# Attention of a two-layer decoder trunk: the join of two head groups in two later parts, weight casts tied behind attention casts, long scans placed behind a turn

## The chip, the cores and the metric

The kernel runs on one core of one Trainium2 chip. The metric is the device time of one execution in microseconds; the number for the kernel before is the median of three runs.

## What is computed

Two layers; each adds to the residual stream x (1024 tokens, 1024 features) first a mixer and then a gated feed-forward part, and a final normalisation follows. All arithmetic is float32.

```python
h = rmsnorm(x, norm1[l]); proj = h @ w_in[l]
qa, ka, va, qb, kb, vb, gate_pre = jnp.split(proj, splits, axis=-1)
o_a = dilated_mixture(...)            # 3 groups of 4 heads of 64: windows 128, 512, 2048, dilations 1, 4, 16
o_b = stick_breaking_attention(...)   # 4 heads of 64
gates = jax.nn.sigmoid(gate_pre + b_gate[l])
merged = g_a * (o_a @ w_br[l, :OUT_A]) + g_b * (o_b @ w_br[l, OUT_A:])
x = x + merged @ w_o[l]
h2 = rmsnorm(x, norm2[l]); up = h2 @ w_up[l]; a, v = up[..., :D_FF], up[..., D_FF:]
x = x + (gelu(causal_depthwise_conv(a)) * v) @ w_down[l]
```

Per head slot the three groups of the first mixer are combined with weights proportional to their softmax denominators. The stick-breaking attention weighs key s for query t with sigmoid(z_ts) times the product of (1 - sigmoid(z_tj)) over all j between s and t; a query block of 128 rows needs a scan along its keys.

## The kernel before

**Products.** A float32 operand is split into a high part (a cast on ACT, line 130) and a low part (source less high part, on DVE, line 135); `split` does both. A product takes three matmuls: high by high, high by low, low by high. The larger projections (`pair`, `up`, `down`) use seven block products instead of eight; their weight sums are made on POOL and DVE and split by `piece`. In `pair` the sums are called w1 to w7, and one step of the generator (a "share") is six matmuls, half of one block product.

**Orders.** PE executes in the order of the program text. For ACT, DVE, POOL and the DMA queue of SP a planner chooses the order when the program is built: it takes what it thinks ready, by priority, which falls in program order; `tc.high_priority(offset=AHEAD)` moves instructions 200 places ahead, and a dependency NO_SYNC fixes the order of two instructions of one engine. Then each engine executes its list strictly in order. `split(..., "is")` remembers the cast just made in `LAST["act"]`, and `split(..., "waits")` puts a cast behind the one remembered. Attention casts are "is" (through `parts`); the casts of the block sums of h are "waits".

**Attention among dense products.** `Dense` holds the dense products of the mixer; `attend` goes through 36 attention items and after each of their steps lets `dense.advance(rate)` issue a number of shares. `dense.at(n, f)` calls f after n more shares. An item has scores, and then pairs of a turn (PE transposes attention weights into a bank of the tag "t", `parts` casts them) and an apply (PE multiplies them with the values into a bank of "o"); `fold` adds the two halves of an o bank into SBUF. The scores of the next item are placed among the turns and applies of the current one, every `gap` places. Every tag of PSUM banks (ps, s, t, o) has two banks.

- B items (`stick_item`), 16 per layer, named by pair and index: two score blocks of up to 128x1024, a scan (line 639) and a product (line 640) for each, before the first turn.
- N items (`near_item`), 4 per layer: group of dilation 1.
- T items (`far_item`), 16 per layer: the two dilated groups, fused; `score` does a bias-and-minimum on DVE (line 807) and an Exp on ACT (line 808).

**Join.** When the last T item of a pair of heads is applied, `join(pr)` runs at once: 16 transposes spread the factors `fx` over four banks (two of "t", then two of "o"), and DVE does six 128x512 operations (lines 882 to 884) to combine the near and the far outputs in `on`. After the second join the remaining dense shares run (`dense.finish`), then the branch products (`br_ps`) with their gates (`gin`, line 1275); the output weights, then the branch weights, go through the two buffers of the tag "wr".

Of the kernel before, what the change touches and what calls it, by code (L numbers as in the profile page):

```python
# [15 lines left out]
P = 128  # L16
# [29 lines left out]
AHEAD_B = 3  # L46
X_AT = (3, 5, 7, 9)
AHEAD = 200


def f32(ap):
# [4 lines left out]
def trunk_kernel(ctx, tc, x, norm1, w_in, b_gate, w_br, w_o, norm2, w_up, conv_w, conv_b, w_down, norm_f, out, depth=None, probe=None):  # L56
# [70 lines left out]
    def split(hi, lo, src, turn=None):  # L127


        one = act.copy(hi, src)  # L130
# [4 lines left out]
        dve.tensor_tensor(lo, src, f32(hi), ALU.subtract)  # L135


    def weights(src, cols, place=None):
# [177 lines left out]
    def attend(dense, items):  # L316

        late = None  # L320
        for i, (name, first, rest, rate, make) in enumerate(items):
            if i == 0:
                dense.until(first)
                dense.step()
                dense.step()
                sc, micro = make()
                for f in sc:
                    f()
                    dense.advance(rate)
                dense.done.add(name + "s")  # L330
            dense.until(rest)
            seq = []
            for m, (t, p) in enumerate(micro):
                seq.append(t)
                if m == 0 and late:
                    seq.append(late)
                if m >= 1:
                    seq.append(micro[m - 1][1])

            def late(f=micro[-1][1], name=name):  # L340
                f()
# [12 lines left out]
            if pending or i + 1 == len(items):  # L354
                seq.append(late)
                late = None
            gap = max(1.0, len(seq) * 0.7 / max(1, len(nxt)))
            at = 0.0
            for j, f in enumerate(seq):
                if nxt and j >= at:  # L360
                    nxt.pop(0)()
                    at += gap
                    if not nxt:
                        dense.done.add(items[i + 1][0] + "s")
                    dense.advance(rate)
# [12 lines left out]
            micro = nmicro  # L378
# [233 lines left out]
            dve.tensor_tensor(dst, o[0:64, :], tmp[0:64, :n], ALU.add)  # L612


    def stick_item(pr, s, qp):
        if "ob" not in R:
            R["ob"] = big("ob")
        q, k, vt, ob = R["qb", pr], R["kb", pr], R["vb"], R["ob"]
        hd = 2 * pr + s
        rows, st, shared = {}, {}, {}  # L620

        def score(a):
            i = 2 * qp + a
            L = P * (i + 1)
            bt = rows[a] = sb.tile([P, T], F32, tag="p4", bufs=4, name="beta")
            if a == 0:
                st[0] = big("stay")
            sv = st[0][:, a, :]
            for c0 in range(0, L, 512):
                w = min(512, L - c0)  # L630
                z = bank("s", "z")
                scores(z[:, :w], *(t[:, s, i * P : i * P + P] for t in q), k[:, s, c0 : c0 + w])
                with tc.high_priority(offset=AHEAD):
                    if c0 + w == L:
                        dve.tensor_tensor(z[:, w - P : w], z[:, w - P : w], mask_b, ALU.add)
                    act.activation(bt[:, c0 : c0 + w], z[:, :w], AF.Sigmoid)
                    act.activation(sv[:, c0 : c0 + w], z[:, :w], AF.Sigmoid, scale=-1.0)  # L637
            rev = sv[:, 0:L][:, ::-1]
            dve.tensor_tensor_scan(rev, rev, zero[:, 0:1].to_broadcast([P, L]), 1.0, ALU.mult, ALU.add)  # L639
            dve.tensor_tensor(bt[:, 0 : L - 1], bt[:, 0 : L - 1], sv[:, 1:L], ALU.mult)  # L640

        def blocks(kb):

            return [(j, a) for j in range(2) for a in range(2) if kb + j <= 2 * qp + a]

        def turn(kb):
            tp = bank("t", "sb_t")
            todo = blocks(kb)
            for c, (j, a) in enumerate(todo):
                pe.transpose(tp[:, c * P : c * P + P], rows[a][:, (kb + j) * P : (kb + j + 1) * P], ident)  # L650
            shared[kb] = parts(tp, len(todo) * P, "sb")

        def apply(kb):
            last = kb == 2 * qp
            if kb == 0:
                shared["o"] = bank("o", "sb_o")[:, :256]
            o = shared["o"]
            for j in range(2):
                c = P if last and j else 0
                for p in (0, 1):  # L660
                    pe.matmul(
                        o[:, c:256],
                        vt[(kb + j) // 4][:, (kb + j) % 4, hd, :],
                        shared[kb][p][:, 256 * j : 256 * j + 256 - c],
                        start=(kb == 0 and j == 0 and p == 0),
                        stop=(last and j == 1 and p == 1),
                        skip_group_check=True,
                    )
# [106 lines left out]
    def far_item(dense, pr, s, r, share):  # L775
# [8 lines left out]
        def score():  # L784
# [15 lines left out]
            for n in range(2):  # L800
                flat = pt[:, 256:768] if n else pt[:, 0:256]
                if n:
                    zz, pp, bb = z1, flat, bias.rearrange("p g c -> p (g c)")
                else:
                    zz, pp, bb = z0[:, 0:256].rearrange("p (g c) -> p g c", g=2), flat.rearrange("p (g c) -> p g c", g=2), bias[:, :, P:256]
                nm = st[:, 0, s, n, r : r + 1]
                dve.tensor_tensor_reduce(pp, zz, bb, 1.0, 3e38, ALU.add, ALU.min, nm)
                act.activation(flat, flat, AF.Exp, bias=nm, scale=-1.0, accum_out=st[:, 1, s, n, r : r + 1])
            if (s, r) == (1, 3):
                factors(pr)  # L810

# [8 lines left out]
        def apply(g):  # L820
# [9 lines left out]
            if r % 2 == 1 and g == 1:  # L830
# [1 line left out]
                    R["ot", pr] = sb.tile([P, T], F32, tag="ot", name="ot")  # L832
                fold(R["ot", pr][64 * s : 64 * s + 64, 512 * (r // 2) : 512 * (r // 2) + 512], o)
                if s == 1 and r == 3:
                    join(pr)

        return [score], [(lambda g=g: turn(g), lambda g=g: apply(g)) for g in range(2)]

# [26 lines left out]
                pool.tensor_copy(fx[:, :, :, s, :], f[:, a, s, :, :].unsqueeze(3).to_broadcast([P, 2, 4, 64]))  # L865
            R["fx", pr].append(fx.rearrange("p n r s c -> p n r (s c)"))

    def join(pr):

        fx, on, ot = R["fx", pr], R["on"], R["ot", pr]  # L870
        spread = []
        for n in range(2):
            for a in range(2):
                o = bank("to"[n], "j_ps")
                for r in range(4):
                    pe.transpose(o[:, r * P : (r + 1) * P], fx[a][:, n, r, :], ident)
                spread.append(o.rearrange("p (r j) -> p r j", r=4))
        mine = on[:, pr, :].rearrange("p (n j r) -> p n r j", n=2, r=4)
        other = ot.rearrange("p (r n j) -> p n r j", r=4, n=2)
        for n in range(2):  # L880
            t = small("jn").rearrange("p (r j) -> p r j", r=4)
            dve.tensor_tensor(t, other[:, n], spread[2 * n + 1], ALU.mult)
            dve.tensor_tensor(mine[:, n], mine[:, n], spread[2 * n], ALU.mult)
            dve.tensor_tensor(mine[:, n], mine[:, n], t, ALU.add)


    def half(n, k):
        return [(H[n][0][:, 4 * k + i, :], H[n][1][:, 4 * k + i, :]) for i in range(4)]

    def piece(src):  # L890
        hi = sb.tile([P, 512], F32R, tag="wh", bufs=4, name="w_hi")
        lo = sb.tile([P, 512], F32R, tag="wl", bufs=4, name="w_lo")
        split(hi, lo, src)
        return hi, lo

    def seven(o, w, b, first, last):
# [65 lines left out]
    def pair(dense, l, offs, tiled, put):  # L962
# [23 lines left out]
        w1 = piece(a11)  # L986
        yield
        dve.tensor_tensor(a11, a21, a11, ALU.subtract)
        w5 = piece(a21)
        yield  # L990
        w6 = piece(a11)
        yield
        pool.tensor_tensor(a11, a12, a11, ALU.subtract)
# [932 lines left out]
```

## Time and profile before

| | |
|---|---|
| median of three runs | 2705.64 us (2704.53 to 2706.54) |
| the profiled execution | 2705.66 us, its span 2703.6 us |
| PE busy | 2663.9 us, 99% |
| PEld, DVE, ACT, POOL busy | 83%, 74%, 50%, 25% |
| mean granted clock of PE | 0.996 |

The page groups instructions by line, engine and tiles ("out<-in"); "idle before, releaser" tells how long the engine sat idle before them and whose end released it. PEld is PE's load of the stationary operand. An L number is a line of the kernel. In the waits, a row is: who waited <- for whom: us in total, times, longest. In a timeline, a row is: start, duration, engine, line, operation, tiles, shapes, count, and in brackets the idle time before it. The two layers run the same program, the second some 1340 us after the first, so most rows of the attention come twice.

### The profile page before, as it was taken

The numbers are of one execution on the slowest core, as the hardware profiler recorded it, in microseconds if no ns is written. First come the engines' busy times: TensorE is split into PE (matmuls) and PEld (weight loads), VectorE is DVE, ScalarE is ACT, GpSimd is POOL, SyncE is SP. The second block draws the span as 40 slices with busy tenths as digits, with TensorE's granted clock in tenths as the row PEclk, the third lists the DMA queues.
The fourth block names the chain that finished last, engine by engine and source line by source line (L and its number), as shares of the span: only waits on it lengthen the run. The fifth ranks groups of instructions, "written<-read, shape, count | busy, mean of one in ns | idle before, by whom it ended". The sixth has DMA issues, their size and how long they took to land.

```text
span 2703.6 us, 36629 instructions
## 1 busy us (share of the span) xinstructions
PE 2663.9 (99%) x13104; PEld 2236.2 (83%) x13104; DVE 2012.4 (74%) x2974; ACT 1351.8 (50%) x2494; POOL 673.2 (25%) x487
## 2 busy tenths in 40 slices
PE   9999999999999999999999999999999999999999
PEld 8988888888888888888888888888788888888888
DVE  5776855675789988897657767466848888988865
ACT  5655645464555555532335556455635555454225
POOL 1003221122233434321120042211311433343210
PEclk9999999999999999999999999999999999999999
DMA  5112178563235444688411122784722443446863
GB/s 161 32 52 94 45 192 244 190 234 110 86 117 171 141 156 142 221 324 315 167 36 40 48 90 75 206 250 162 251 86 78 151 160 136 169 145 252 335 244 122
DMA packets 358690, 421.05 MB, mean 156 GB/s; under 512 B 20732, under 2 KB 287340, under 8 KB 356972
## 3 DMA queue, kind: packets, MB, share of 16 engines
q1 hardware_dynamic: 358508, 418.70, 46.7%
q8 instruction: 104, 1.70, 0.3%
q14 instruction: 78, 0.64, 0.1%
HBM read 278.59 MB, written 140.05 MB: 155 GB/s over the span
## 4 chain that ended last, share of the span: by engine, by line
PE 82%; DVE 10%; issue 2%; ACT 2%; DMA 1%; POOL 1%; SPq 0%; DVEq 0%; POOLq 0%; ACTq 0%
PE u_a L899 5%; PE u_a L901 5%; PE u_a L900 5%; PE d_ps L1622 4%; PE d_ps L1624 4%; PE d_ps L1623 4%; PE u_c L901 3%; PE u_c L899 3%; PE u_c L900 3%; PE o_ps L160 2%; PE o_ps L162 2%; PE o_ps L161 2%; PE i_a L899 2%; PE i_a L900 2%; PE i_a L901 2%
## 5 line engine op out<-in xcount | busy, mean ns | idle before, releaser
L135 DVE TENSOR_TENSOR w_lo<-up_a,w_hi 128x512 fp32r<-128x512 f32 x240 | 237.6, 997 | 21.3 <-ACT w_hi L130 21.3
L130 ACT CAST w_hi<-up_a 128x512 fp32r<-128x512 f32 x240 | 149.4, 622 | 185.2 <-PE u_a L900 45.3
L1630 DVE TENSOR_TENSOR x<-x,d_ps 128x512 f32<-128x512 f32 (+1 forms) x228 | 152.0, 672 | 77.7 <-PE d_ps L1624 76.4
L1361 POOL TENSOR_TENSOR cv<-cv 128x512 f32<-128x512 f32 x88 | 132.3, 1515 | 249.4 <-DVE cv L1356 139.6
L135 DVE TENSOR_TENSOR g<-cv,g 128x512 fp32r<-128x512 f32 x154 | 152.6, 992 | 5.3 <-ACT g L130 2.7
L135 DVE TENSOR_TENSOR w_lo<-w_raw,w_hi 128x512 fp32r<-128x512 f32 x148 | 112.2, 761 | 58.0 <-ACT w_hi L130 57.4
L130 ACT CAST w_hi<-w_raw 128x512 fp32r<-128x512 f32 x148 | 91.9, 621 | 121.7 <-PE o_ps L161 69.7
L135 DVE TENSOR_TENSOR w_lo<-in_a,w_hi 128x512 fp32r<-128x512 f32 x120 | 86.1, 718 | 70.5 <-ACT w_hi L130 70.1
L130 ACT CAST w_hi<-in_a 128x512 fp32r<-128x512 f32 x120 | 74.5, 621 | 124.2 <-PE i_c L900 49.2
L1622 PE MATMUL d_ps<-gd_in,w_hi 128*128 128x512 f32 (+1 forms) x340 | 130.5, 384 | 1.7 <-issue 0.8
L1623 PE MATMUL d_ps<-gd_in,w_hi 128*128 128x512 f32 (+1 forms) x340 | 129.8, 382 | 0.0
L1624 PE MATMUL d_ps<-gd_in,w_lo 128*128 128x512 f32 (+1 forms) x340 | 129.8, 382 | 0.0
L899 PE MATMUL u_a<-hh,w_hi 128*128 128x512 f32 x320 | 124.6, 390 | 1.5 <-DVE u L1512 1.5
L900 PE MATMUL u_a<-hl,w_hi 128*128 128x512 f32 x320 | 124.5, 389 | 0.0
L901 PE MATMUL u_a<-hh,w_lo 128*128 128x512 f32 x320 | 124.5, 389 | 0.0
L900 PE MATMUL u_a<-t_lo,w_hi 128*128 128x512 f32 x320 | 124.5, 389 | 0.0
L901 PE MATMUL u_a<-t_hi,w_lo 128*128 128x512 f32 x320 | 124.5, 389 | 0.0
L899 PE MATMUL u_a<-t_hi,w_hi 128*128 128x512 f32 x320 | 124.5, 389 | 0.0
L639 DVE TENSOR_TENSOR_SCAN stay<-stay,zero 128x128 f32<-128x128 f32 (+3 forms) x64 | 86.9, 1358 | 42.6 <-ACT stay L637 42.5
L1622 PE MATMUL d_ps<-gd_in,wd 128*128 128x512 f32 (+1 forms) x292 | 113.9, 390 | 0.0
L130 ACT CAST g<-cv 128x512 fp32r<-128x512 f32 x154 | 94.9, 616 | 37.3 <-POOL cv L1361 29.8
L1624 PE MATMUL d_ps<-gd_in,wd 128*128 128x512 f32 (+1 forms) x292 | 112.8, 386 | 0.0
(404 smaller groups left out, 8632.8 us busy)
## 6 DMA issues: line engine op xcount, KB each, us to landing
gd<-g SPq DMA_DIRECT2D x154, 512.0 KB, 3.7
gd_in<-gd SPq DMA_DIRECT2D x154, 512.0 KB, 6.2
up_a<-in_w_up_dram SPq DMA_DIRECT2D x80, 512.0 KB, 4.9
t_kq<-tk SPq DMA_DIRECT2D x32, 768.0 KB, 4.8
wd_raw<-in_w_down_dram SPq DMA_DIRECT2D x22, 1024.0 KB, 11.1
w_raw<-in_w_in_dram SPq DMA_DIRECT2D x80, 256.0 KB, 2.9
in_a<-in_w_in_dram SPq DMA_DIRECT2D x40, 512.0 KB, 5.3
gin<-gs SPq DMA_DIRECT2D x32, 512.0 KB, 4.3
```

Of the source, the lines that this page charges most:

```text
L130: one = act.copy(hi, src)
L135: dve.tensor_tensor(lo, src, f32(hi), ALU.subtract)
L160: pe.matmul(o, lh, rh, start=(first and i == 0), stop=False, skip_group_check=share)
L639: dve.tensor_tensor_scan(rev, rev, zero[:, 0:1].to_broadcast([P, L]), 1.0, ALU.mult, ALU.add)
L899: pe.matmul(o, w[0][:, c], rh, start=(first and i == 0), stop=False, skip_group_check=True)
L900: pe.matmul(o, w[0][:, c], rl, start=False, stop=False, skip_group_check=True)
L901: pe.matmul(o, w[1][:, c], rh, start=False, stop=(last and i == 3), skip_group_check=True)
L1361: return lambda: pool.tensor_tensor(dst, a, b, ALU.subtract)
L1622: pe.matmul(o[:, sub], wh[:, c], gh[:, sub], start=(i == 0 and k in (0, 4, 5)), stop=False, skip_group_check=True)
L1623: pe.matmul(o[:, sub], wh[:, c], gl[:, sub], start=False, stop=False, skip_group_check=True)
L1624: pe.matmul(o[:, sub], wl[:, c], gh[:, sub], start=False, stop=(i == m - 1), skip_group_check=True)
L1630: dve.tensor_tensor(x, x, o[:, sub], ALU.add)
```

## The change

- `split` with "is" also remembers the low part's instruction in `LAST["dve"]`.
- The scores of the next item are placed every 0.5 (was 0.7) of the places per score.
- A B item no longer scans at the end of its score: block, weights and length go into the list `SCANS`. `scans()` issues what is in it: at once for lengths up to 512, else at the start of an item's first turn and behind the casts of every turn. Each scan is put behind `LAST["dve"]` on DVE.
- The minimum and the Exp of the far scores get the high priority.
- `join` issues nothing itself; it sets half 0 (two banks of "t") two shares later and half 1 (two banks of "o") `JOIN` = 4 shares later, each with its eight transposes and three DVE operations.
- `piece` passes a turn on, and w5, w3 and w7 of `pair` are split with "waits".

```diff
+JOIN = 4
...
-        dve.tensor_tensor(lo, src, f32(hi), ALU.subtract)
+        two = dve.tensor_tensor(lo, src, f32(hi), ALU.subtract)
+        if turn == "is":
+            LAST["dve"] = two.ins.name
...
-            gap = max(1.0, len(seq) * 0.7 / max(1, len(nxt)))
+            gap = max(1.0, len(seq) * 0.5 / max(1, len(nxt)))
...
+    SCANS = []
...
-            rev = sv[:, 0:L][:, ::-1]
-            dve.tensor_tensor_scan(rev, rev, zero[:, 0:1].to_broadcast([P, L]), 1.0, ALU.mult, ALU.add)
-            dve.tensor_tensor(bt[:, 0 : L - 1], bt[:, 0 : L - 1], sv[:, 1:L], ALU.mult)
+            SCANS.append((bt, sv, L))
+            if L <= 512:
+                scans()
+
+        def scans():
+
+            for bt, sv, L in SCANS:
+                rev = sv[:, 0:L][:, ::-1]
+                one = dve.tensor_tensor_scan(rev, rev, zero[:, 0:1].to_broadcast([P, L]), 1.0, ALU.mult, ALU.add)
+                if "dve" in LAST:
+                    tc.add_manual_dep(one.ins, LAST["dve"], NO_SYNC, reason="in turn")
+                dve.tensor_tensor(bt[:, 0 : L - 1], bt[:, 0 : L - 1], sv[:, 1:L], ALU.mult)
+            SCANS.clear()
...
         def turn(kb):
+            if kb == 0:
+                scans()
             tp = bank("t", "sb_t")
...
             shared[kb] = parts(tp, len(todo) * P, "sb")
+            scans()
...
-                dve.tensor_tensor_reduce(pp, zz, bb, 1.0, 3e38, ALU.add, ALU.min, nm)
-                act.activation(flat, flat, AF.Exp, bias=nm, scale=-1.0, accum_out=st[:, 1, s, n, r : r + 1])
+                with tc.high_priority(offset=AHEAD):
+                    dve.tensor_tensor_reduce(pp, zz, bb, 1.0, 3e38, ALU.add, ALU.min, nm)
+                    act.activation(flat, flat, AF.Exp, bias=nm, scale=-1.0, accum_out=st[:, 1, s, n, r : r + 1])
...
-    def join(pr):
+    def join(dense, pr):
...
-        spread = []
-        for n in range(2):
+        mine = on[:, pr, :].rearrange("p (n j r) -> p n r j", n=2, r=4)
+        other = ot.rearrange("p (r n j) -> p n r j", r=4, n=2)
+
+        def half_of(n):
+            spread = []
             for a in range(2):
                 o = bank("to"[n], "j_ps")
                 for r in range(4):
                     pe.transpose(o[:, r * P : (r + 1) * P], fx[a][:, n, r, :], ident)
                 spread.append(o.rearrange("p (r j) -> p r j", r=4))
-        mine = on[:, pr, :].rearrange("p (n j r) -> p n r j", n=2, r=4)
-        other = ot.rearrange("p (r n j) -> p n r j", r=4, n=2)
-        for n in range(2):
             t = small("jn").rearrange("p (r j) -> p r j", r=4)
-            dve.tensor_tensor(t, other[:, n], spread[2 * n + 1], ALU.mult)
-            dve.tensor_tensor(mine[:, n], mine[:, n], spread[2 * n], ALU.mult)
+            dve.tensor_tensor(t, other[:, n], spread[1], ALU.mult)
+            dve.tensor_tensor(mine[:, n], mine[:, n], spread[0], ALU.mult)
             dve.tensor_tensor(mine[:, n], mine[:, n], t, ALU.add)
+
+        dense.at(2, lambda: half_of(0))
+        dense.at(JOIN, lambda: half_of(1))
...
-        w5 = piece(a21)
+        w5 = piece(a21, "waits")
...
-        w3 = piece(a11)
+        w3 = piece(a11, "waits")
...
-        w7 = piece(u2)
+        w7 = piece(u2, "waits")
```

More of the change, by code (lines that the diff above doesn't have):

```diff
@@ L834, in apply @@
                 if s == 1 and r == 3:
-                    join(pr)
+                    join(dense, pr)
         return [score], [(lambda g=g: turn(g), lambda g=g: apply(g)) for g in range(2)]
@@ L877, in join, with piece @@
                 spread.append(o.rearrange("p (r j) -> p r j", r=4))
-        mine = on[:, pr, :].rearrange("p (n j r) -> p n r j", n=2, r=4)
-        other = ot.rearrange("p (r n j) -> p n r j", r=4, n=2)
-        for n in range(2):
             t = small("jn").rearrange("p (r j) -> p r j", r=4)
-            dve.tensor_tensor(t, other[:, n], spread[2 * n + 1], ALU.mult)
-            dve.tensor_tensor(mine[:, n], mine[:, n], spread[2 * n], ALU.mult)
+            dve.tensor_tensor(t, other[:, n], spread[1], ALU.mult)
+            dve.tensor_tensor(mine[:, n], mine[:, n], spread[0], ALU.mult)
             dve.tensor_tensor(mine[:, n], mine[:, n], t, ALU.add)
+        dense.at(2, lambda: half_of(0))
+        dense.at(JOIN, lambda: half_of(1))
     def half(n, k):
         return [(H[n][0][:, 4 * k + i, :], H[n][1][:, 4 * k + i, :]) for i in range(4)]
-    def piece(src):
+    def piece(src, turn=None):
         hi = sb.tile([P, 512], F32R, tag="wh", bufs=4, name="w_hi")
         lo = sb.tile([P, 512], F32R, tag="wl", bufs=4, name="w_lo")
-        split(hi, lo, src)
+        split(hi, lo, src, turn)
         return hi, lo
```

## The prediction

> **What bounds the kernel.** I read the page first, then the waits of PE, then stretches of the granted clock, then the timelines around the longest waits.
>
> ```profile
> span 2703.6 us, 36629 instructions
> PE 2663.9 (99%) x13104; PEld 2236.2 (83%) x13104; DVE 2012.4 (74%) x2974; ACT 1351.8 (50%) x2494; POOL 673.2 (25%) x487
> PE 82%; DVE 10%; issue 2%; ACT 2%; DMA 1%; POOL 1%; SPq 0%; DVEq 0%; POOLq 0%; ACTq 0%
> ```
>
> PE bounds the kernel: it is busy for 2663.9 of 2703.6 us. The diff adds, removes and resizes no matrix product; it moves work in time. So at most the 39.7 us in which PE idles, plus time lost to a lowered clock, can be had. Which waits are they? The waits of PE over the whole span:
>
> ```profile
> PE sb_o L661 <- DVE sbl L135: 5.1, 2, 2.7
> PE j_ps L876 <- DVE ot L612: 4.8, 4, 1.7
> PE z L596 <- DVE st L807: 3.4, 2, 2.0
> PE br_ps L160 <- DVE gin L1275: 2.7, 2, 2.5
> PE o L725 <- DVE p0l L135: 2.2, 2, 1.1
> PE o L825 <- DVE p1l L135: 2.0, 6, 0.7
> PE o L825 <- ACT p1h L130: 1.2, 2, 0.6
> ```
>
> (Total us, times, longest.) These seven make 21.4 us, all in the attention or just behind it, each occurring in both layers. The rest of the idle time lies at the start and in stages that the diff leaves alone.
>
> A wait can cost more than its length. Stretches of 3.41 us, two at a time; the last three numbers of a row are the granted clock, the DMA share and GB/s:
>
> ```profile
> 145.88:149.29 3.41, 0.94 (x7) 0.74 (x6) 3.18 (x5) 0.48 (x1) 0.00 (x0) 1.00 0.17 65
> 149.30:152.71 3.41, 3.41 (x14) 2.82 (x12) 0.30 (x1) 0.24 (x2) 0.00 (x0) 0.50 0.25 72
> 459.91:463.32 3.41, 3.41 (x11) 2.73 (x10) 0.66 (x2) 1.65 (x5) 2.55 (x2) 0.50 0.77 220
> 565.72:569.12 3.40, 1.70 (x12) 1.32 (x11) 3.34 (x5) 2.24 (x4) 0.00 (x0) 1.00 0.99 346
> 569.13:572.54 3.41, 3.41 (x17) 2.79 (x16) 3.41 (x6) 2.18 (x5) 0.00 (x0) 1.00 0.70 282
> 1487.32:1490.73 3.41, 3.41 (x13) 2.86 (x12) 0.30 (x1) 0.32 (x2) 0.00 (x0) 0.50 0.25 71
> 1924.23:1927.63 3.40, 3.40 (x9) 2.64 (x8) 3.09 (x4) 0.62 (x1) 1.93 (x2) 0.50 0.85 253
> ```
>
> A stretch in which PE works 0.94 us is followed by one at clock 0.50; a stretch with 1.70 us of work is followed by full clock. Four stretches at 0.50 stand behind waits of 2.0 us and more; each costs half of 3.41, so 1.7 us, together 6.8 us. A wait that only shrinks below some 1.7 us saves this too.
>
> The Trainium skill ("TensorE: Matmul & The Clock Gate", "Why this matters for your kernels") asks only that no idle gap exceed about 3 us, one idle window being what returns the clock to half. No wait in the table reaches 3 us, and the clock fell four times: here the measurement decides. By that rule the sum below would lose 6.8 us of its gain and end at 2695.1.
>
> **The change part by part.** (1) *Long scans behind a turn; the second score earlier.* The wait of 2.5 us at 148.69 and what DVE did before it:
>
> ```profile
> 141.83 0.69 DVE L135 TENSOR_TENSOR sbl<-sb_t,sbh 128x512 fp32r<-128x512 f32 x1
> 142.43 0.29 DVE L635 TENSOR_TENSOR z<-z,mask_b 128x128 f32<-128x128 f32 x1
> 143.87 2.29 DVE L639 TENSOR_TENSOR_SCAN stay<-stay,zero 128x1024 f32<-128x1024 f32 x1 [1.15 <-ACT stay L637]
> 146.20 1.22 DVE L640 TENSOR_TENSOR beta<-beta,stay 128x1023 f32<-128x1023 f32 x1
> 147.34 0.69 DVE L135 TENSOR_TENSOR w_lo<-w_raw,w_hi 128x512 fp32r<-128x512 f32 x1
> 147.95 1.15 DVE L135 TENSOR_TENSOR sbl<-sb_t,sbh 128x512 fp32r<-128x512 f32 x2
> 148.69 0.38 PE L661 MATMUL sb_o<-sbl,vb 128*128 128x256 f32 x1 [2.47 <-DVE sbl L135]
> ```
>
> PE waits for a cast's low part that stands behind scan, product and a weight's low part (2.29 + 1.22 + 0.69 = 4.2 us), while DVE had idled 1.15 us ahead of the scan. With gap 0.5 instead of 0.7 the second score of the next item is asked for at place 2 instead of 3 of eight, ahead of the turn; its mask can go before the turn's cast, and that cast (0.69) fills part of the idle 1.15. The scan then starts about 0.7 to 1.15 earlier, and the next cast has only scan and product before it if the weight's part is passed (0.69 more). So 2.47 falls to between 0 and 1.8; I take 0.8, nearest to 2.47 less 1.15 and less half a microsecond of luck with the weight's part. The wait in layer 2 is the 2.7 of the table: 5.1 - 1.6 = 3.5, plus two clock stretches 3.4: **-6.9** (bounds 0 and -8.5). What a scan is placed behind is asked for earlier by PE's own order, so it waits for nothing new; behind it on DVE stand its product and lower-priority work, and the turn that reads it comes an item later.
>
> (2) *High priority for the far scores.* The place where PE waits 2.0 us for a score bank:
>
> ```profile
> 456.77 0.69 DVE L135 TENSOR_TENSOR w_lo<-in_a,w_hi 128x512 fp32r<-128x512 f32 x1 [1.83 <-ACT w_hi L130]
> 457.39 0.69 DVE L1044 SCALAR_TENSOR_TENSOR kq_l<-i_a,kq_h 128x512 fp32r<-128x512 f32 x1
> 458.00 0.41 DVE L807 CUSTOM_DVE_ANT_1 p<-z,bias 128x256 f32<-128x256 f32 x1
> 458.48 0.33 PE L596 MATMUL z<-t_kq 128*128 128x128 f32 x1 [1.99 <-DVE st L807]
> ```
>
> In order, DVE stood at a weight's low part, then did the key's; the score came third. Priority lets it pass the key's low part (0.69), hardly the first, which the planner had thought ready earlier. The key's part then goes to DRAM 0.7 us later, off the path. 2 x 0.7 and one clock stretch: **-3.1** (bounds 0, if the order stays, and -3.4 - 1.7 = -5.1).
>
> (3) *Weight casts tied behind attention casts.* Ahead of the first join:
>
> ```profile
> 488.85 0.62 ACT L130 CAST w_hi<-in_a 128x512 fp32r<-128x512 f32 x1 [3.84 <-POOL in_a L993]
> 490.39 0.39 PE L825 MATMUL o<-p1h,t_v 128*128 128x256 f32 x1 [0.58 <-ACT p1h L130]
> 491.13 0.39 PE L825 MATMUL o<-p1l,t_v 128*128 128x256 f32 x1 [0.36 <-DVE p1l L135]
> ```
>
> ACT stood idle 3.84 us before a weight cast (w3) that POOL had to release, with the attention cast behind it. w3 is written behind that turn, so the tie turns the two round: 0.94 per layer, **-1.9** (bounds 0 and -3.2, both o L825 rows). Behind the tied cast wait the weight's low part and a product three products on, 36 matmuls later, so it is covered; without that cover each tie would cost the cast's 0.62. The p0l waits (2.2 us) have the block sums before them on DVE, which no tie reaches: 0.
>
> (4) *The join in two parts.* Its 16 transposes stay; today they run as 12 and 4, then as 8 and 8. The last four now wait for the fold of the same item, the 4.8 us of the table, because they need both o banks at once and DVE does a join product before the fold. Two and four shares later the fold is long done and dense products stand between: **-4.8** (bounds -2.7, if the first join's later banks bind, and -4.8). No DMA is in it, but its two fx tiles are freed up to 5.5 us later (four shares of six products), so a gate tile in SP's queue that takes their place starts that much later; POOL has only the fx copies, ahead of all this.
>
> New is who waits for the banks. Per half DVE does:
>
> ```profile
> L883 DVE TENSOR_TENSOR on<-on,j_ps x8: 1090/1106/1154, 492.2 to 1903.7; 128x512 f32<-128x512 f32 x8
> L882 DVE TENSOR_TENSOR jn<-ot,j_ps x8: 666/685/692, 495.0 to 1905.3; 128x512 f32<-128x512 f32 x8
> ```
>
> Both banks are free 1.8 us after the transposes if DVE comes at once. The first join's banks go next to the next pair's turn and fold; I put 0.5 per layer there, and 1.0 for scores that come more densely: **+2.0** (bounds 0 and 2 x 1.8 + 2 = 5.6).
>
> (5) *What follows the second join*, in layer 2:
>
> ```profile
> 1903.90 0.60 ACT L130 CAST w_hi<-w_raw 128x512 fp32r<-128x512 f32 x1
> 1907.85 0.68 DVE L135 TENSOR_TENSOR w_lo<-w_raw,w_hi 128x512 fp32r<-128x512 f32 x1
> 1913.89 5.03 SPq L1228 DMA_DIRECT2D br_raw<-in_w_br_dram  x2
> 1920.59 1.14 ACT L130 CAST br_w<-br_raw 128x512 fp32r<-128x512 f32 x2 [7.15 <-DMA br_raw<-in_w_br_dram]
> 1923.19 0.50 PE L160 MATMUL br_ps<-oh_a,br_w 128*128 128x512 f32 x1 [2.52 <-DVE gin L1275]
> ```
>
> The wait of 2.52 us ends a chain of buffers: w_lo frees the slot of the second output weight, that one frees the branch weight's, whose arrival DVE waits for with the gate product behind it. w_lo waited 3.4 us behind the undivided join. Split, the join leaves DVE free right after the fold, so w_lo comes up to 3.4 earlier; PE comes 1.0 earlier too. If the chain gains 2, the wait is 1.5 and the clock holds: -1.0 - 1.7 = **-2.7** (bounds +1.0, chain unmoved, and -4.2).
>
> Sum: -6.9 - 3.1 - 1.9 - 4.8 + 2.0 - 2.7 = **-17.4 us**. The profiled execution took 2705.66 us (span 2703.6 and 2.06 around it), the median is 2705.64: 2688.3 us.
>
> **The rivals.** *Orders stay.* The planner places instructions by when it thinks them ready; if (1), (2) and (5) leave the orders as they are, only joins and ties remain: -4.8 - 1.9 + 2.0 = -4.7, 2701.0. For it: the idle 1.83 in (2), where priority has nothing to choose from. Against: the diff forces the scan's order.
>
> *Slower: the scan behind one cast stands ahead of the next.* The place is DVE in the longest items, one 1024-wide scan per item, four a layer:
>
> ```profile
> L639 DVE TENSOR_TENSOR_SCAN stay<-stay,zero 128x1024 f32<-128x1024 f32 x4 | 9.2, 2292 | 3.9 <-ACT stay L637 3.9
> ```
>
> Each such place can lose what the one above loses, 2.5 and 1.7 for the clock, 4.2 us. Now two of eight do. If all do, (1) is gone and six are new: 2688.3 + 6.9 + 25.2 = 2720.4; from three new ones on (2707.8) it is slower than before. For it: the tie forbids DVE to scan while a turn is late. Against: six places have slack today, and the score is asked for earlier.
>
> *The chain of (5) doesn't move* and PE meets it earlier by what the joins gave, 1.0 in layer 2 and up to 1.7 (the longest j_ps wait) in layer 1: -17.4 + 2.7 + 2.7 = -12.0, 2693.6.
>
> *The clock holds through waits of 2 us*, so that removing them gives no 6.8: 2695.1. The four rows at 0.50 speak against it. It is the Trainium skill's rule above.
>
> **How the numbers follow.** Forecast 0.56; orders stay 0.16; slower 0.16; chain 0.10; clock 0.02. A measurement can tell 0.2%, 5.4 us. Faster by more: 0.56 + 0.10 + 0.02 and 0.06 of the orders' case, which lies at the edge: 0.74. Within: its other 0.10. Slower: 0.16. The forecast's own range is 2680 (every part at its better bound: -8.5 - 5.1 - 3.2 - 4.8 - 4.2 = -25.8) to 2697 ((1) and (2) at half, the new waits at 5.6: -8.8); 2680 to 2708 takes in the chain and the orders' case and leaves out most of the slower one.
>
> **What would show it.** Right: the sb_o wait under 1.8 us and PE's clock at 1.00 after the start; no j_ps wait; the p1h wait at the first join gone; the far score ahead of the key's low part. Wrong: several sb_o waits in the long items (the slower rival), a wait of t or o L825 on a join product, br_ps waiting longer than 2.5 us.

## The result, and the profile after

The kernel after takes 2695.67 us (median of 7 runs, 2693.63 to 2700.21) against 2704.88 us of the kernel before beside it (7 runs, 2701.45 to 2706.54). The ratio is 0.9971, 95% interval 0.9961 to 0.9980: 7.8 us less, between 5.4 and 10.5. The forecast was 17.4 us less.

The page of the kernel after, and then its waits of PE (us in total, times, longest). Its profiled execution took 2700.21 us, the longest of the seven.

```profile
span 2698.4 us, 36609 instructions
PE 2662.5 (99%) x13104; PEld 2233.0 (83%) x13104; DVE 2017.0 (75%) x2974; ACT 1352.6 (50%) x2494; POOL 672.1 (25%) x487
```

```profile
PE br_ps L163 <- DVE gin L1297: 8.0, 4, 3.7
PE sb_o L679 <- DVE sbl L136: 4.3, 4, 1.7
PE o L743 <- DVE p0l L136: 2.7, 3, 1.2
...
PE z L599 <- DVE st L826: 2.4, 3, 1.4
...
PE o L844 <- DVE p1l L136: 1.1, 3, 0.7
...
PE sb_t L667 <- DVE beta L654: 0.5, 2, 0.2
```

Beside the list of before: the j_ps wait (4.8) is gone, and so is the p1h wait (1.2); sb_o fell from 5.1 to 4.3, z from 3.4 to 2.4. One wait grew much, and it is now the longest: **br_ps, from 2.7 to 8.0 us**. What the parts of the change gave, the branch products behind the attention took back in good part. (The 8.0 is that of the longest of the seven executions: the traces of the five kernels below that keep the joins and what follows them as changed have 5.5 to 7.5.)

The stretches of the clock around three of the longest waits of after, the first of sb_o and that of br_ps in each layer (busy time of PE, PEld, DVE, ACT, POOL; then granted clock, DMA share, GB/s):

```profile
146.02:149.43 3.41, 1.72 (x11) 1.36 (x9) 2.44 (x4) 0.48 (x1) 0.00 (x0) 1.00 0.20 60
149.43:152.84 3.41, 3.41 (x23) 3.04 (x22) 1.63 (x5) 1.23 (x4) 0.00 (x0) 1.00 0.08 25
572.69:576.09 3.40, 1.48 (x6) 1.24 (x7) 2.46 (x5) 2.59 (x5) 0.00 (x0) 1.00 0.69 242
576.10:579.50 3.40, 3.40 (x12) 2.71 (x10) 1.29 (x2) 0.00 (x0) 0.00 (x0) 0.50 0.52 181
1907.30:1910.70 3.40, 0.66 (x3) 0.57 (x4) 2.58 (x4) 3.19 (x6) 0.00 (x0) 1.00 0.49 164
1910.71:1914.11 3.40, 3.40 (x10) 2.61 (x9) 0.69 (x1) 0.78 (x3) 0.00 (x0) 0.50 1.01 342
```

Three of the four stretches at half clock are gone: the two behind sb_o and the one behind z. The branch products now have two, one in each layer, where they had one. So two fewer in all, worth 3.4 us by the prediction's price. (PE's busy time, which holds the slow stretches, fell by 1.4 us only, 2663.9 to 2662.5; what filled the other 2.0 is open.)

Why does PE wait for the gate product in layer 1, where it waited 0.2 us before (the list's 2.7 less its longest, 2.5)? The timeline of after (start, duration, engine, line, operation, tiles, shapes, count, idle time before):

```profile
566.80 0.37 SPq L1250 DMA_DIRECT2D br_raw<-in_w_br_dram  x1
...
569.45 1.09 DVE L902 TENSOR_TENSOR on<-on,j_ps 128x512 f32<-128x512 f32 x1
570.43 0.71 DVE L136 TENSOR_TENSOR ol_a<-on,oh_a 128x512 fp32r<-128x512 f32 x1
...
572.04 1.31 DVE L136 TENSOR_TENSOR br_w<-br_raw,br_w 128x512 fp32r<-128x512 f32 x2
...
573.24 0.72 DVE L136 TENSOR_TENSOR ol_a<-on,oh_a 128x512 fp32r<-128x512 f32 x1
573.85 1.31 DVE L1297 TENSOR_TENSOR gin<-gin,br_ps 128x512 f32<-128x512 f32 x2
574.61 0.50 PE L163 MATMUL br_ps<-oh_b,br_w 128*128 128x512 f32 x1 [2.52 <-DVE gin L1297]
```

The third branch product needs the bank that the first gate product (line 1297) reads. On DVE that product stands behind the second half of the join, two low parts of `ol_a` and two low parts of branch weights. The branch weight's load was issued at 566.80; before it was issued here:

```profile
577.27 0.38 SPq L1228 DMA_DIRECT2D br_raw<-in_w_br_dram  x1
...
578.04 0.69 DVE L1275 TENSOR_TENSOR gin<-gin,br_ps 128x512 f32<-128x512 f32 x1 [0.80 <-PE br_ps L162]
```

There DVE had nothing else to do and stood waiting for the branch product. After, the load is issued 10.5 us earlier on the clock of the execution. 7.3 us of that are PE's own, for its first branch product starts at 569.21 instead of 576.48; measured from that product the load is 3.2 us earlier. So the weight's low parts are in DVE's queue ahead of work that PE needs sooner.

Layer 2 in the kernel after; PE's first branch product is the row at 1903.50:

```profile
1899.72 0.38 SPq L148 DMA_DIRECT2D w_raw<-in_w_o_dram  x1
1900.56 0.32 SPq L1242 DMA_DIRECT2D gin<-gs  x1
...
1902.35 0.37 SPq L1242 DMA_DIRECT2D gin<-gs  x1
...
1903.50 0.39 PE L163 MATMUL br_ps<-oh_b,br_w 128*128 128x512 f32 x1
...
1906.92 0.62 ACT L131 CAST w_hi<-w_raw 128x512 fp32r<-128x512 f32 x1 [5.55 <-DMA w_raw<-in_w_o_dram]
...
1907.57 0.69 DVE L136 TENSOR_TENSOR w_lo<-w_raw,w_hi 128x512 fp32r<-128x512 f32 x1 [2.50 <-ACT w_hi L131]
...
1909.31 1.28 DVE L1297 TENSOR_TENSOR gin<-gin,br_ps 128x512 f32<-128x512 f32 x2
...
1910.05 0.50 PE L163 MATMUL br_ps<-oh_b,br_w 128*128 128x512 f32 x1 [3.66 <-DVE gin L1297]
```

Here the gate product stands behind the output weight's low part on DVE, and that one waits for ACT, which waits 5.55 us for the weight's load. From its issue to that cast 7.2 us went by; before, 3.6:

```profile
1902.72 2.03 SPq L1220 DMA_DIRECT2D gin<-gs  x2
...
1908.56 0.38 SPq L145 DMA_DIRECT2D w_raw<-in_w_o_dram  x1
...
1912.20 0.62 ACT L130 CAST w_hi<-w_raw 128x512 fp32r<-128x512 f32 x1 [0.98 <-DMA w_raw<-in_w_o_dram]
...
1912.35 0.39 PE L160 MATMUL br_ps<-oh_b,br_w 128*128 128x512 f32 x1
```

The DMA share during the load, of before and then of after (one stretch each):

```profile
1908.56:1912.20 3.64, 3.64 (x18) 3.02 (x17) 3.58 (x6) 2.62 (x5) 0.00 (x0) 1.00 0.60 200
```

```profile
1899.72:1906.92 7.20, 6.66 (x34) 5.28 (x32) 5.36 (x7) 0.62 (x1) 0.00 (x0) 1.00 0.96 369
```

The load did not move against PE: it is issued 3.8 us ahead of PE's first branch product in both kernels (1908.56 and 1912.35, 1899.72 and 1903.50). The two gate loads moved. Before, both were issued 4 us and more ahead of the weight's load; after, they come 0.8 and 2.6 us behind it. Their tiles (`gin`) share the tag "p4" with the tiles `fx`, and the second half of the join is the last to read `fx`. A half that comes later gives these buffers free later.

The other traces bear this out. In after and in those five (no_scan, scan_now, gap07, no_prio, no_tie) the weight's load is issued 3.8 us ahead of PE's first branch product, the gate loads come behind it, and it takes 5.5 to 7.2 us up to the cast. In before, join_at_once and join2_at_once the gate loads are 4 us ahead of it, and it takes 3.1 to 4.7.

### The profile page after: what moved, and what is told of

It is laid out like the page before. It is cut to its first block, busy times and chain, and to the rows that moved or that the text cites. A ratio compares the mean times of both kernels' runs of the same rounds, so it can differ in the third digit from the quotient of the medians.

```text
span 2698.4 us, 36609 instructions
## 1 busy us (share of the span) xinstructions
PE 2662.5 (99%) x13104; PEld 2233.0 (83%) x13104; DVE 2017.0 (75%) x2974; ACT 1352.6 (50%) x2494; POOL 672.1 (25%) x487
## 4 chain that ended last, share of the span: by engine, by line
PE 84%; DVE 8%; issue 2%; ACT 2%; DMA 2%; POOL 0%; SPq 0%; DVEq 0%; ACTq 0%; POOLq 0%
PE u_a L921 5%; PE u_a L922 5%; PE u_a L923 5%; PE d_ps L1644 5%; PE d_ps L1645 5%; PE d_ps L1646 5%; PE u_c L921 3%; PE u_c L922 3%; PE u_c L923 3%; PE i_a L921 2%; PE i_a L922 2%; PE i_a L923 2%; PE o_ps L163 2%; PE o_ps L164 2%; PE o_ps L165 2%
## 5 line engine op out<-in xcount | busy, mean ns | idle before, releaser
L1644 PE MATMUL d_ps<-gd_in,wd 128*128 128x512 f32 (+1 forms) x292 | 113.9, 390 | 0.0
L1646 PE MATMUL d_ps<-gd_in,wd 128*128 128x512 f32 (+1 forms) x292 | 112.8, 386 | 0.0
L1645 PE MATMUL d_ps<-gd_in,wd 128*128 128x512 f32 (+1 forms) x292 | 112.8, 386 | 0.0
```

The lines of the kernel that those rows point to most:

```text
L1644: pe.matmul(o[:, sub], wh[:, c], gh[:, sub], start=(i == 0 and k in (0, 4, 5)), stop=False, skip_group_check=True)
L1645: pe.matmul(o[:, sub], wh[:, c], gl[:, sub], start=False, stop=False, skip_group_check=True)
L1646: pe.matmul(o[:, sub], wl[:, c], gh[:, sub], start=False, stop=(i == m - 1), skip_group_check=True)
```

## The experiments

The theory, after the two traces were compared: parts (1) to (4) gave most of what was forecast, and (5) turned round. The late halves of the second join make the gate product late: on DVE in layer 1, through the output weight's load in layer 2. The rivals: a part other than (5) fell short; or the branch wait comes from the denser scores or the ties, not from the late halves of the join. Each kernel is compared with the kernel before beside it.

| kernel | edit on the kernel after | median, us | ratio to before (95%) |
|---|---|---|---|
| after | none | 2695.67 | 0.9971 (0.9961 to 0.9980) |
| join_at_once | both joins undivided in time | 2697.22 | 0.9976 (0.9967 to 0.9985) |
| join2_at_once | second join at once | 2697.21 | 0.9971 (0.9960 to 0.9982) |
| join2_1_2 | second join 1 and 2 shares later | 2691.11 | 0.9951 (0.9939 to 0.9964) |
| gates_first | later work tied behind the first gate product | 2699.47 | 0.9983 (0.9974 to 0.9992) |
| no_scan | part (1) undone | 2701.65 | 0.9990 (0.9981 to 0.9998) |
| scan_now | gap 0.5, scans at once | 2696.00 | 0.9970 (0.9959 to 0.9982) |
| gap07 | gap 0.7, scans behind a turn | 2699.83 | 0.9991 (0.9982 to 1.0000) |
| no_prio | part (2) undone | 2699.83 | 0.9975 (0.9965 to 0.9985) |
| no_tie | part (3) undone | 2697.06 | 0.9974 (0.9965 to 0.9983) |
| prod_late_j12 | join2_1_2, and long products one turn later | 2685.94 | 0.9939 (0.9926 to 0.9951) |
| all_three | prod_late_j12 and gates_first | 2692.23 | 0.9958 (0.9944 to 0.9971) |

0.0010 is 2.7 us, and an interval reaches some 2.5 to 3.5 us to either side. The difference of two ratios is then known to about 0.0013 to 0.0018 (an estimate from these intervals), and kernels that lie closer are not told apart by time; there only the waits speak. Each trace is of one execution, and its waits are those of that execution.

### join_at_once: part (4) undone

```diff
-        dense.at(2, lambda: half_of(0))
-        dense.at(JOIN, lambda: half_of(1))
+        half_of(0)
+        half_of(1)
```

> The kernel after, but both halves of the join are issued at once, in both pairs (part 4 undone whole; all else as after). Theory A (the two halves, placed two and four shares later, are what put the gate product behind other work): the waits for br_ps fall from 8.0 us to those of before, about 2.7 (0.2 in layer 1, 2.5 in layer 2); one of the two half-clock stretches goes (1.7); the four waits for j_ps of together about 4.8 come back. 2695.7 + 4.8 - 5.3 - 1.7 = about 2693.5, so within 3 us of the kernel after. Rival B (something else of the change, such as the denser scores or the ties, delays the gate product): br_ps stays at 6 to 8 us, j_ps comes back, about 2700.5.

Its waits of PE:

```profile
PE j_ps L898 <- DVE ot L615: 4.8, 4, 1.7
...
PE br_ps L163 <- DVE gin L1297: 1.7, 2, 1.5
```

The waits are theory A's: j_ps is back with 4.8, br_ps falls from 8.0 to 1.7, and no stretch at half clock stands behind the branch products. So the late halves, not the scores or the ties, brought the branch wait. The time, 2697.22, lies between the two forecasts; against the kernel after it is 0.0005, 1.4 us, which can't be told from nothing. (The spans of the two traces differ by 6.0 us, but the one is of the longest execution of its kernel, the other of the shortest.) The split of the join, forecast at -4.8 + 2.0 and up to 2.7 more, was worth about nothing as a whole.

### join2_at_once and join2_1_2: only the second join moved

```diff
-        dense.at(2, lambda: half_of(0))
-        dense.at(JOIN, lambda: half_of(1))
+        if pr:
+            half_of(0)
+            half_of(1)
+        else:
+            dense.at(2, lambda: half_of(0))
+            dense.at(JOIN, lambda: half_of(1))
```

> The kernel after, its second join issued at once as before; the first join stays in two later parts. Theory A (the later half of the second join puts its three DVE operations, and what is ordered around them, ahead of the gate products): the br_ps wait of layer 1 goes from 2.5 us to under 0.5 and its clock stretch with it, that of layer 2 from 5.4 in all back to about 2.5; the j_ps waits of the second join come back with 1.7 and 1.0. Sum against the kernel after: -4.2 + 1.7 in layer 1, -2.9 + 1.0 in layer 2, about -4.4 us. Rival B (PE only meets the buffer chain of the output and branch weights earlier, whatever the join does): br_ps stays at 2 us or more in layer 1, and the time rises by the 2.7 us of j_ps.

```diff
-        dense.at(2, lambda: half_of(0))
-        dense.at(JOIN, lambda: half_of(1))
+        dense.at(1 if pr else 2, lambda: half_of(0))
+        dense.at(2 if pr else JOIN, lambda: half_of(1))
```

> The kernel after, the halves of the second join one and two shares later instead of two and four. Theory A: no j_ps wait over 0.3 us, the second half's DVE work is done 2.7 us earlier, so br_ps waits under 1 us in layer 1 at full clock and at most 2.5 in layer 2; about -6 us against the kernel after. Rival B: br_ps as in the kernel after (2.5 and 5.4 us, two stretches at half clock), time the same.

With the second join at once, br_ps is 1.7 in all (three waits, the longest 1.3) and 2.8 of the 4.8 us of j_ps are back. The time does not fall below that of after: a miss for the time that was expected, though the waits came as theory A has them. With one and two shares there is no j_ps wait, and br_ps is short:

```profile
PE br_ps L163 <- DVE gin L1297: 1.3, 2, 0.9
```

The time falls to 0.9951, 5.4 us under after. Two shares cover the fold of the item; the further two were not needed for that, and they pushed the gate product back. DVE's order in layer 1 of join2_1_2:

```profile
570.81 0.69 DVE L1297 TENSOR_TENSOR gin<-gin,br_ps 128x512 f32<-128x512 f32 x1
572.19 0.69 DVE L136 TENSOR_TENSOR br_w<-br_raw,br_w 128x512 fp32r<-128x512 f32 x1 [0.69 <-ACT br_w L131]
```

The gate product now stands ahead of the branch weights, 2.2 us behind PE's first branch product instead of 4.6. In layer 2 the output weight's low part now stands behind the first gate product, so that a late load no longer holds it.

### gates_first: the order on DVE forced

```diff
+        elif turn == "gate" and "gate" in LAST:
+            tc.add_manual_dep(two.ins, LAST["gate"], NO_SYNC, reason="behind the first gate product")
...
-        next(wo[0])
         next(residual, None)
...
+            if (i, ab) == (0, 1):
+                LAST["gate"] = gated_.ins.name
+                next(wo[0])
```

The low parts of `ol_a`, of the later branch weights and of the output weights are cast with the turn "gate", and the output weight asked for ahead of the branch products is asked for after the first one.

> The kernel after, in which DVE may do the low parts of the branch input of the second mixer part (ol_a), of the later branch weights and of the output weights only behind the first gate product; the output weights are asked for one branch product later. The join stays as changed (two and four shares). It tells apart what in the later half of the second join costs. Theory A1 (DVE's order: the gate product stands behind work that is ahead of it in the list): br_ps in layer 1 falls from 2.5 to under 1 us at full clock, in layer 2 from 3.7 to under 1 at that place. Theory A2 (the freed slots of the fx tiles and the weights' DMAs come too late): br_ps stays at 2 us or more at the same place, and with the output weights later the waits behind grow. Under A1 too a later br_ps wait may grow by the branch weights that come later, 1 to 3 us.

The wait at the third branch product is gone in both layers, as theory A1 has it: PE waited there for the order on DVE. But the time did not fall: the ratio is 0.0012 above after's, 3.2 us, which is not quite told from nothing. PE waits elsewhere:

```profile
PE x_t L1153 <- ACT gin L1247: 3.7, 1, 3.7
```

This wait is not in after's list; ACT stood there waiting for a gate load. Another 2.8 us are left at later branch products. An order that is right for one wait was paid for further on.

### no_scan, scan_now and gap07: part (1) and its two halves

no_scan undoes part (1):

```diff
-            gap = max(1.0, len(seq) * 0.5 / max(1, len(nxt)))
+            gap = max(1.0, len(seq) * 0.7 / max(1, len(nxt)))
...
-            if L <= 512:
-                scans()
+            scans()
...
-                if "dve" in LAST:
-                    tc.add_manual_dep(one.ins, LAST["dve"], NO_SYNC, reason="in turn")
```

> The kernel after without its part on the scans: scans at the end of each score again, no order behind the cast, gap 0.7. Theory (the part took 0.8 us and a stretch of half clock, 1.7 us, out of each layer, and gave back 0.25 + 0.3 per layer in new small waits): sb_o 2.5 and 2.7 us again with the clock at 0.50 behind each, the two sb_t waits of 0.25 gone, about +4 us. Rival (the gain of the change comes from the join and the ties alone): the same time within 1 us.

The two long sb_o waits return, 5.1 in all and 2.6 at the longest, a stretch at half clock behind each, and so do the two g_ps waits of 0.5. By ratio part (1) is worth 0.0019, 5.1 us.

scan_now keeps the gap of 0.5 and takes only the last two of the edits above; gap07 takes only the first.

> The kernel after with the gap of 0.5 kept, but scans issued at once at the end of the score and not tied behind a cast. Theory A (the gap decides): sb_o stays at about 1.7, no new waits for g_ps, sb_t waits of 0.25 gone; 2695.7 less 0.5, within 2 us. Rival B (the tie decides): sb_o 2.5 twice with a half-clock stretch behind each, about 2700.5, like the version with the whole part undone (2701.7).

> The kernel after with the gap of 0.7 again (second score of an item asked for later); scans still behind a turn. Theory A (the gap decides: the mask goes ahead of the turn's cast, so the scan starts earlier): the two long waits for sb_o return to 2.0 to 2.5 us with half a clock stretch behind each: 1.6 + 3.4, about 2700.5. Rival B (the tie decides: the scan may no longer overtake the cast): sb_o stays at 1.7 or less, and the time at 2695.7 within 2 us.

scan_now is as fast as after (0.9970) with sb_o waits of 1.6 us at the longest and no half clock behind them: **as far as can be told, the whole gain of part (1) comes from the gap, and the scans placed behind a turn give nothing measurable**. With gap07 the time is that of theory A, but not its wait. The cast passes the scan, as the tie demands, and the wait moves on to the transposes that read the product:

```profile
PE sb_t L667 <- DVE beta L654: 6.0, 5, 1.5
...
PE sb_o L679 <- DVE sbl L136: 0.7, 2, 0.3
```

DVE in gap07, at the place that the prediction showed:

```profile
142.55 0.69 DVE L136 TENSOR_TENSOR sbl<-sb_t,sbh 128x512 fp32r<-128x512 f32 x1
143.15 0.29 DVE L640 TENSOR_TENSOR z<-z,mask_b 128x128 f32<-128x128 f32 x1
...
146.08 0.69 DVE L136 TENSOR_TENSOR sbl<-sb_t,sbh 128x512 fp32r<-128x512 f32 x1 [0.28 <-ACT sbh L131]
146.68 2.28 DVE L651 TENSOR_TENSOR_SCAN stay<-stay,zero 128x1024 f32<-128x1024 f32 x1
```

The mask stands behind the cast, and the tie puts the scan behind one cast more, so that it starts at 146.68. scan_now, which has no tie, has the mask ahead:

```profile
142.11 0.29 DVE L640 TENSOR_TENSOR z<-z,mask_b 128x128 f32<-128x128 f32 x1
142.31 0.68 DVE L136 TENSOR_TENSOR sbl<-sb_t,sbh 128x512 fp32r<-128x512 f32 x1
143.55 2.29 DVE L650 TENSOR_TENSOR_SCAN stay<-stay,zero 128x1024 f32<-128x1024 f32 x1 [0.56 <-ACT stay L642]
```

DVE idles 0.56 us before the scan, as in after; in before and in no_scan, with the mask behind the cast, it idles 1.15. A step of the prediction holds: the mask ahead of the cast brings the scan forward, and the cast fills part of the idle time.

### no_prio and no_tie: parts (2) and (3) undone

```diff
-                with tc.high_priority(offset=AHEAD):
-                    dve.tensor_tensor_reduce(pp, zz, bb, 1.0, 3e38, ALU.add, ALU.min, nm)
-                    act.activation(flat, flat, AF.Exp, bias=nm, scale=-1.0, accum_out=st[:, 1, s, n, r : r + 1])
+                dve.tensor_tensor_reduce(pp, zz, bb, 1.0, 3e38, ALU.add, ALU.min, nm)
+                act.activation(flat, flat, AF.Exp, bias=nm, scale=-1.0, accum_out=st[:, 1, s, n, r : r + 1])
```

> The kernel after without the high priority of the far scores. Theory (priority lets the score pass the key's low part only): z waits of 2.0 and 1.4 us again, one stretch at half clock, about +2.9 us. Rival (the order is the same without it): the same time.

The z waits are 4.0 in all (two, the longest 2.0) instead of 2.4, but no stretch at half clock follows them. The stretches around the first:

```profile
453.25:456.66 3.41, 2.15 (x14) 1.75 (x12) 1.58 (x3) 1.22 (x2) 1.74 (x1) 1.00 0.82 201
456.67:460.07 3.40, 2.69 (x16) 2.31 (x17) 2.40 (x9) 2.48 (x7) 1.55 (x2) 1.00 0.82 226
```

A wait of 2 us fell across the border of two stretches, and in each PE still worked more than 2 us. In the kernel before, the same wait lay in one. So the clock's 1.7 us in part (2) came or went with the run. The ratio differs from after's by 0.0004, which can't be told from nothing.

For part (3) the three weight sums are split without "waits":

```diff
-        w5 = piece(a21, "waits")
+        w5 = piece(a21)
...
-        w3 = piece(a11, "waits")
+        w3 = piece(a11)
...
-        w7 = piece(u2, "waits")
+        w7 = piece(u2)
```

> The kernel after with w5, w3 and w7 no longer tied behind attention casts. Theory (the tie turns one weight cast and one attention cast round ahead of each first join): the o <- p1h waits of 0.6 and p1l of 0.4 us come back in both layers, +1.9 us, nothing else changes. Rival (the join in two parts alone removed them, since dense products now stand between): those waits stay away, the same time within 0.5 us.

```profile
PE o L844 <- DVE p1l L136: 1.8, 5, 0.7
PE o L844 <- ACT p1h L131: 1.5, 2, 0.9
```

These two are 3.3 us against 1.1 in after: the ties take 2.2 us of waits away. The time differs by 0.0003, less than can be told.

### prod_late_j12 and all_three: the version that beats both

In the prediction the first sb_o wait was to fall to 0.8; it fell to 1.70, with the scan's product still ahead of the cast. So the product of the long blocks is put off too:

```diff
+            todo, PRODUCTS[:] = PRODUCTS[:], []
+            for bt, sv, L in todo:
+                one = dve.tensor_tensor(bt[:, 0 : L - 1], bt[:, 0 : L - 1], sv[:, 1:L], ALU.mult)
+                tc.add_manual_dep(one.ins, LAST["dve"], NO_SYNC, reason="in turn")
             for bt, sv, L in SCANS:
...
-                dve.tensor_tensor(bt[:, 0 : L - 1], bt[:, 0 : L - 1], sv[:, 1:L], ALU.mult)
+                if L == T:
+                    PRODUCTS.append((bt, sv, L))
+                else:
+                    dve.tensor_tensor(bt[:, 0 : L - 1], bt[:, 0 : L - 1], sv[:, 1:L], ALU.mult)
...
-        dense.at(2, lambda: half_of(0))
-        dense.at(JOIN, lambda: half_of(1))
+        dense.at(1 if pr else 2, lambda: half_of(0))
+        dense.at(2 if pr else JOIN, lambda: half_of(1))
```

> The kernel with the second join's halves one and two shares later, in which besides the product (line 640 before) behind a scan of the full 1024 columns waits for the low part of the next turn's cast. Theory (what is left of sb_o, 1.70 us per layer, is the product's 1.22 ahead of the cast): sb_o falls to about 0.5 in both layers and the 0.44 of the second pair to 0, so -3.3 us against that kernel. Rival (the scan itself and the weight's low part hold the cast): sb_o stays over 1.2 us, the same time.

DVE in prod_late_j12:

```profile
143.49 2.29 DVE L655 TENSOR_TENSOR_SCAN stay<-stay,zero 128x1024 f32<-128x1024 f32 x1 [0.56 <-ACT stay L642]
...
146.28 0.68 DVE L136 TENSOR_TENSOR sbl<-sb_t,sbh 128x512 fp32r<-128x512 f32 x1
146.88 1.22 DVE L651 TENSOR_TENSOR beta<-beta,stay 128x1023 f32<-128x1023 f32 x1
```

```profile
PE sb_o L686 <- DVE sbl L136: 1.5, 2, 0.8
```

The cast is ahead of the product, and the sb_o waits fall from 4.3 to 1.5 us. At 2685.94 us and ratio 0.9939 this is the fastest version, 16.5 us under the kernel before. By the ratios it is 3.2 us under join2_1_2; their intervals overlap, and for these 3.2 the waits speak.

all_three adds the edit of gates_first.

> The three together: second join one and two shares later, product behind the next cast, gate product first. If the parts add up: 2691 - 3.3 and up to 1 less at br_ps, 2687 us. If the gate product first only moves the wait to the branch weights: 2688 to 2691.

It is 0.0019 slower than prod_late_j12, 5.1 us, and slower than both forecasts. With the second join at one and two shares the gate product is no longer late; the tie puts the low parts of `ol_a` back, and PE now waits 2.0 us for them.

## Why the prediction was wrong

The direction was right, and the size was not: 7.8 of 17.4 us. By the prediction's steps, from the two profiled executions:

| step | forecast | waits and clock, before to after | by undoing it |
|---|---|---|---|
| (1) scans, scores | -6.9 | sb_o -0.8, g_ps -0.9, sb_t +0.5, two stretches -3.4: -4.6 | -5.1 |
| (2) far scores | -3.1 | z 3.4 to 2.4, -1.0; a stretch -1.7: -2.7 | -1.1, not told from 0 |
| (3) ties | -1.9 | p1h 1.2 and p1l 2.0 to 1.1: -2.1 | -0.8, not told from 0; waits -2.2 |
| (4) join, its own wait | -4.8 | j_ps: -4.8 | waits -4.8 |
| new waits for banks | +2.0 | none on a join product; p0l 2.2 to 2.7: +0.5 | p0l 3.0 in join_at_once, so not the banks |
| (5) branch chain | -2.7 | br_ps 2.7 to 8.0, +5.3; one more stretch +1.7: **+7.0** | in join_at_once: waits 8.0 to 1.7, -6.3; two stretches -3.4 |

The middle column sums to -6.7; the spans of the two profiled executions differ by 5.2, and the medians, by their ratio, by 7.8. The row of (5) is that of one long execution, so its +7.0 need not be that of the median.

**The step that failed is (5).** It forecast -2.7 with bounds of +1.0 and -4.2, and the traces show +7.0. By time, 5.4 of the missing 9.6 us come back when the second join is put off by one and two shares only. The failing sentence is "If the chain gains 2, the wait is 1.5 and the clock holds". It took the gate product to be held by the branch weight's arrival alone, so that an earlier weight had to mean an earlier product.

In layer 2, whose rows the step was worked out from, the chain gained nothing on PE. `w_lo` starts 4.5 us ahead of PE's first branch product in both kernels, for on DVE it still waits 2.5 us, the first half of the join among what stands ahead, where it had waited 3.4. What came later against PE are the gate loads. Part (4) had seen this ("a gate tile in SP's queue that takes their place starts that much later") and put no price on it. They met the output weight's load, which took 7.2 us instead of 3.6, and the gate product stands behind that weight on DVE. In layer 1 the chain did gain, 3.2 us, and the gain was part of the trouble. On an engine that works in order, an operation whose input comes earlier can be placed ahead of one that is needed sooner: the branch weight's low parts (1.31 us) stood ahead of the gate product, with the second half of the join and its `ol_a`.

join_at_once, join2_at_once and join2_1_2 show that the late halves of the second join cause the longer wait. In time only join2_1_2 shows it; the other two pay the j_ps wait in its place. Two things stay open, for neither was tried by itself: which of the two halves does it, and whether the gate loads alone make the weight's load slow.

Two smaller misses lie in (1). The sb_o wait fell to 1.70, not 0.8; with the scan's product (1.22) put off in prod_late_j12 the longest is 0.8. And the scans placed behind a turn, which the rival "slower" rested on, give and cost nothing that can be told at gap 0.5; that rival did not occur.

**New waits** at +2.0 were too high for the attention: no wait of PE stands on a join product. The price of the split stood elsewhere, in the branch products.

**The rivals.** "Orders stay" did not occur: the mask and the far score both changed places. "The chain doesn't move" (-12.0) holds for layer 2 by its premise: the chain kept its distance to PE. But its price, 1.0 us more at the same product, is not what came; PE now waits at the third branch product instead of the seventh, and for another reason. Its time, 2693.6, is nearer to the measured one than the forecast's by luck. "The clock holds" is refuted by the stretch at 0.50 behind the wait of 2.52 us.

## What to carry to other kernels

Splitting a step and putting it later removes the wait in front of it, but what it used to hold back may come forward, it itself lands among later work, and the buffers that it reads come free later: follow all three on each in-order engine and in each DMA queue up to the next operation that the bound engine waits for. Measure "earlier" from the bound engine's own work, for in the second layer everything is earlier by what was gained before. Put a step off only as far as its cover needs; here two shares gave 5 us that four shares had lost. Where a wait goes through an engine's order, try the edit that brings the producer forward (here the gap) apart from the one that forces the order (here the tie), for one of them may do all the work.

## What the runs showed of the hardware

The half clock is decided in fixed stretches of 3.41 us. In the kernel before the stretches at 0.50 begin at 149.30, 459.91, 1487.32 and 1924.23; the distances from the first are 91.0, 392.0 and 520.0 times 3.413. The Trainium skill ("TensorE: Matmul & The Clock Gate", "What's actually happening") says that the window is 3413 ns long and free-running; these distances agree.

So what counts is how much PE works inside one such stretch, not how long a wait is: 0.66 and 1.48 us of work led to half clock, 1.72 did not, and a wait of 2 us across a border was followed by none. The limit between the two is not sharp in these traces. gates_first has a stretch with 1.95 us of work (1913.44 to 1916.85) that was followed by half clock. no_scan has two with 1.88 and 1.87 us (from 325.73 and from 1663.76); the first was followed by it and the second was not. The borders lie differently against the kernel's own work from one execution to the next: the first long sb_o wait ends at 148.69 in before and at 148.74 in no_scan, and the half clock behind it begins at 149.30 and at 148.24. So a wait of 2 us at the far scores was followed by half clock in before and not in no_prio.

A 256-KB load took 3.6 us up to the cast that waits for it at a DMA share of 0.60, and 7.2 us at 0.96, with two gate loads of 512 KB issued 0.8 and 2.6 us behind it. A load that is issued at the same distance ahead of PE need not land at the same distance.
